# The first norms of a streaming-encoder layer: token sums by one-column matmuls instead of 512-column ones and VectorE additions

## The chip, the cores and the metric

The kernel runs on one core of a Trainium2 chip. The metric is the device time of one execution in microseconds. Three runs of the kernel before took 2073.66 (the median), 2082.34 and 2072.43 us.

## The reference

One layer on 1024 tokens of width 1024, all in float32. It is a first gated feed-forward block, a mixing block (latent attention beside an RWKV-7 recurrence) and a second feed-forward block, each ahead of it with a norm that is modulated by a conditioning vector, and a last norm. What matters here is the start:

```python
mod = silu(c) @ w_mod + b_mod                  # 9 vectors of 1024: sh1, sc1, gt1, ...
u = modulate(rmsnorm(x, ffn1_norm_g), sh1, sc1)
h = x + 0.5 * gt1 * swiglu(u, ffn1_w_gate, ffn1_w_up, ffn1_w_down)

rmsnorm(x, g):  x * rsqrt(mean(x * x, over the 1024 channels) + 1e-6) * g
modulate(u, shift, scale):  u * (1 + scale) + shift
```

The norm needs one number per token: the root of the mean square over the channels.

## The kernel before

Activations lie with channels on the partitions: 8 tiles of 128 channels (index d), each cut into two halves of 512 tokens (index a). So the sum of squares of a token runs over the 128 partitions of eight tiles, and its reciprocal root, to be multiplied in, must stand on all partitions: as "rows", 128 x 512, the same in every partition.

**First half (a = 0), `root` from line 1712.** For each tile ScalarE squares it (L1723) and TensorE multiplies the 512 columns of squares by a 128x128 matrix of ones (L1724), adding up in one PSUM bank. The result is the sum of every token on all partitions at once. ScalarE takes the root of the 128x512 (L254), VectorE its reciprocal (L255, 128x512); that is the rows. The squares turn in four scratch tiles (f8 to f11).

**Second half (a = 1).** `SumSq` squares each tile on ScalarE (L204) and adds six of the eight squares into an accumulator on VectorE (L208). `token_sums` (L216) then takes 128 tokens at a time as the stationary operand of a matmul with one column of ones, for the accumulator and the last square: the sums come out one token per partition, as 128x4. Root and reciprocal are on 128x4. `spread` (L221 to L232) multiplies the identity with them (L226, 128x512 on VectorE), lets TensorE multiply that by the ones (L230), and ScalarE copies the result to SBUF (L231): rows again.

**Rows at work, `norm_raw` (L312).** Even tiles are normalized by VectorE (L320) and then ScalarE (L321), odd ones by POOL (L317) and then ScalarE (L318). Each tile is then split into a high and a low part (L61 on ScalarE, L62 on VectorE), and these are the operands of the first feed-forward products (L68). The weights of these products are split in the same way.

**Modulation.** Scale and shift of the first two tiles come from TensorE (`mod_first`, L152 to L163: 32 matmul instructions with a single stationary column, a copy of the row by ScalarE, and its transposition by L160). Those of the other six tiles come from VectorE, one multiplication of 128x1024 for each of twelve vectors (`mod_one`, L140), on tiles of w_mod that DMA brings. `gain` (L186) makes the factor of a tile.

PSUM scratch called "norm" is drawn from banks 6 and 7 in turn. The tile "nr", which holds the rows, has one buffer: the rows of the second half can be written once those of the first are used up.

**Order.** The engines execute in program order, each its own. That order is written when the kernel is built: a planner takes the instructions by their place in the program and by their times in a simulated timeline. Waits are set from the tiles that instructions share.

Of the kernel before, what the change touches and what calls it, by code (L numbers as in the profile page):

```python
# [13 lines left out]
F32 = mybir.dt.float32  # L14
# [3 lines left out]
ALU = mybir.AluOpType  # L18
AX = mybir.AxisListType
# [3 lines left out]
P = 128  # L23
D = 1024
S = 1024
HB = 512
ND = D // P
# [50 lines left out]
def ps(k, name):  # L78
    b = next(k.bank[name])
    return k.psum.tile([P, HB], F32, name="ps_" + name, tag=f"bank{b}", bufs=1)  # L80
# [8 lines left out]
def spare(slots):  # L89

    return itertools.cycle([(*s, D)[:3] for s in slots])
# [14 lines left out]
def vectors(k, pool):  # L106

    nc = k.nc
    k.pv, k.bmod = (k.const.tile([P, k.I[n].shape[1]], F32, name=n) for n in ("pv", "b_mod"))
    nc.scalar.dma_start(out=k.pv, in_=k.I["pv"])  # L110
    nc.scalar.dma_start(out=k.bmod, in_=k.I["b_mod"])
    k.ccol = k.const.tile([P, ND], F32, name="ccol")
    nc.scalar.activation(out=k.ccol, in_=vec(k, "c"), func=AF.Silu)
# [97 lines left out]
def token_sums(k, parts, t, n=HB):  # L211

    for b in range(n // P):
        c = slice(b * P, (b + 1) * P)
        for i, x in enumerate(parts):
            k.nc.tensor.matmul(  # L216
                t[:, b : b + 1], lhsT=x[:, c], rhs=k.ones[:, 0:1], start=i == 0, stop=i == len(parts) - 1
            )


def spread(k, r, bank, out):  # L221

    nc = k.nc
    m = r.shape[1]
    ident = k.ident[:, None, :].broadcast_to([P, m, P])
    nc.vector.tensor_tensor(  # L226
        out=out.rearrange("p (b q) -> p b q", q=P), in0=ident, in1=r[:, :, None].broadcast_to([P, m, P]), op=ALU.mult
    )
    t = ps(k, bank)[:, : m * P]
    nc.tensor.matmul(t, lhsT=k.ones, rhs=out, start=True, stop=True)  # L230
    nc.scalar.copy(out=out, in_=t)  # L231
    return t  # L232
# [19 lines left out]
def root_mean(k, t, n, out):  # L252

    k.nc.scalar.activation(out=out, in_=t, func=AF.Sqrt, scale=1.0 / n, bias=k.eps)  # L254
    k.nc.vector.reciprocal(out=out, in_=out)  # L255


def rstd(k, pool, ss):

    t = ps(k, "norm")  # L260
    m = ss.n // P
    token_sums(k, ss.parts, t, ss.n)
    r = pool.tile([P, 4], F32, name="rt", tag="rt", bufs=2)[:, :m]
    root_mean(k, t[:, :m], D, r)
    rows = pool.tile([P, HB], F32, name="nr", tag="nr", bufs=1)[:, : ss.n]
    return spread(k, r, "norm", rows), rows
# [21 lines left out]
def empty():  # L288
    return [[None, None] for _ in range(ND)]
# [13 lines left out]
def h_tiles(k, pool, a, out, singles=0):  # L303

    for d in range(singles):
        out[d][a] = pool.tile([P, HB], F32, name=f"h{d}_{a}", tag=f"h{d}_{a}")
    for d in range(singles, ND, 2):
        t = pool.tile([P, 2, HB], F32, name=f"h{d}_{a}", tag=f"h{d}_{a}")
        out[d][a], out[d + 1][a] = t[:, 0], t[:, 1]
# [1349 lines left out]
def tile_layer(ctx, tc, I, out):  # L1659
    k = Ctx()  # L1660
    setup(ctx, k, tc, I, out)
    nc = k.nc
# [10 lines left out]
    with pool_("ffn1") as pool:  # L1673
        fs = [(pool, f"f{i}") for i in range(12)]
        h0, h1 = [(pool, f"h{d}_0") for d in range(0, ND, 2)], [(pool, f"h{d}_1", HB) for d in range(6)]
        wide = [(pool, "e"), (pool, "h6_1")]
        k.wide = spare(us)
        k.spare = spare(fs[8:])
        h = empty()
        u = {}  # L1680

        def load_x(a):
            h_tiles(k, pool, a, h, 6 * a)
            for d in range(ND):
                nc.sync.dma_start(out=h[d][a], in_=I["x"][d, :, a * HB : (a + 1) * HB])

        vectors(k, pool)
        load_x(0)
        early = 2
        slices = {}  # L1690

        def load_mods(ds):
            for d in ds:
                for v in (1, 0):
                    if d < early:
                        w = slices[v, d] = tmp(k, "wmod", D)
                        nc.sync.dma_start(out=w.rearrange("p (i q) -> p i q", q=P), in_=I["w_mod_in"][v * ND + d])
                    else:
                        slices[v, d] = mod_loads(k, v, d)

        def mods(d):
            if d < early:
                mod_first(k, d, [slices[v, d] for v in range(2)])
            else:
                for v in (1, 0):
                    mod_one(k, v, d, slices[v, d])
            gain(k, "ffn1_norm_g", 1, slice(d, d + 1))

        load_mods(range(early))
        slots = iter(fs + us)  # L1710

        def root(a):

            if a:
                ss = SumSq(k, pool, nc.vector)
                for d in range(ND):
                    ss.add(h[d][a])
                r = rstd(k, pool, ss)
                return r
            t = ps(k, "norm")  # L1720
            for d in range(ND):
                sq = tmp(k, "nsq")
                nc.scalar.activation(out=sq, in_=h[d][a], func=AF.Square)  # L1723
                nc.tensor.matmul(t, lhsT=k.ones, rhs=sq, start=d == 0, stop=d == ND - 1)  # L1724
            r = pool.tile([P, HB], F32, name="r", tag="nr", bufs=1)
            root_mean(k, t, D, r)
            return r, r

        def normed(a, r):
            for d in range(ND):  # L1730
                if a == 0 and d >= early:
                    mods(d)
                norm_raw(k, r, h[d][a], d, "ffn1_norm_g", 0)
            return [h[d][a] for d in range(ND)]

        r0 = root(0)
        for d in range(early):
            mods(d)
        x = []

        def first_half():
            spread_c(k, pool)
            load_mods(range(early, 4))
            load_x(1)
            load_mods(range(4, ND))
            x.append(normed(0, r0))
            stream_first(k, u, x[0], slots)

        def second_half():
            x.append(normed(1, root(1)))  # L1750
            stream_second(k, u, x[1], us[8:])

        def both():
            stream_sums(k, u, *x, iter(fs[8:] + us))
            k.spare, k.wide = spare(h1), spare(wide)

        def turn(g):
            if g < 0:
                k.spare = spare(wide + h1)
                return  # L1760
            if g == 0:
                banks(k, dn="67012345")
                for a in range(2):
                    load_x(a)
            if g == 3:
                banks(k, in0="012", dn_in1="34", in2="5", norm="67")
                k.spare = spare(fs[8:])

        steps1 = mod_steps(
            k, (2, lambda: half_gate(k, 2)), (4, lambda: gain(k, "mix_norm_g", 4)), (3, None),  # L1770
            (5, None), (7, lambda: gain(k, "ffn2_norm_g", 7)), (6, None), (8, lambda: half_gate(k, 8)),
        )
        steps1 += trig_steps(k, 0) + trig_steps(k, 1)
        steps2 = []

        u2 = empty()
        places = [us[4:12], us[12:] + us[:4]]

        def then(a, r):
            u_tiles(k, places[a], a, u2)  # L1780
            norm_mod(k, pool, r, h, a, "mix_norm_g", 3, u2)
            for d in range(ND):
                nc.sync.dma_start(out=k.hD[a][:, d, :], in_=h[d][a])

        n2 = Normed(k, pool, h, then)
        first, ws = [[], []], []

        def ahead(a, tiles):

            for i in tiles:  # L1790
                if a == 0:
                    ws.append(win_weights(k, pool, I["w_in"][WIN_FIRST[i]], (("raw", 4), ("wo", 8), ("wo", 8))))
                first[a].append(win_mm(k, ws[i], u2, a, "in0" if a == 0 else ("in1", "in1", "in2")[i]))

        ffn(
            k, u, h, I["ffn1_w_gate"], I["ffn1_w_up"], I["ffn1_w_down"], k.mod[:, 2, :], pool, groups(fs, us),
            itertools.chain([wide[0], us[7]], itertools.cycle(h0)), (lambda: None, lambda: (first_half(), second_half()), lambda: None, both), turn, steps1, steps2,
            n2.final, n2.done, [(0, WHOLE), (1, WHOLE)], ahead,
        )
# [33 lines left out]
    with pool_("inv", "left") as ip, pool_("chain") as pool:  # L1833
# [9 lines left out]
        for p in range(NP2):  # L1843
            o = ops.pop(0)
            even, odd, norm, gate = outputs(k, pool, o)
# [25 lines left out]
    h, y, u = empty(), empty(), {}  # L1871
# [3 lines left out]
    pool = Pools((own("h2b"), h0), (own("w2"), ("raw", "f8", "f9", "f10", "f11", "nwy", "nwt")))  # L1875
    us, fs = [(up, f"u{i}") for i in range(16)], [(pool, f"f{i}") for i in range(12)]
# [122 lines left out]
```

## Time and profile before

| | us |
|---|---|
| median of three runs | 2073.66 |
| the profiled execution | 2078.46 |
| its span, first to last instruction | 2076.7 |
| TensorE busy (matmuls) | 1984.3 (96%) |
| VectorE busy | 1537.3 (74%) |
| ScalarE busy | 889.3 (43%) |
| POOL busy | 250.0 (12%) |
| mean granted clock of TensorE | 0.984 |

PE is TensorE's matmuls, PEld its weight loads, DVE is VectorE, ACT ScalarE, POOL GpSimd, SP the engine that issues most DMAs. Of the profiled execution 2076.7 us lie between the first and the last instruction, and the rest is around them. In the profile a float32 matmul stands as two MATMUL and two LDWEIGHTS instructions. Matmuls overlap in the pipeline, so the distance between the starts of two tells more than the duration of one.

### The profile page before, as it was taken

The numbers are of one execution on the slowest core, as the hardware profiler recorded it, in microseconds if no ns is written. First come the engines' busy times: TensorE is split into PE (matmuls) and PEld (weight loads), VectorE is DVE, ScalarE is ACT, GpSimd is POOL, SyncE is SP. The second block draws the span as 40 slices with busy tenths as digits, with TensorE's granted clock in tenths as the row PEclk, the third lists the DMA queues.
The fourth block names the chain that finished last, engine by engine and source line by source line (L and its number), as shares of the span: only waits on it lengthen the run. The fifth ranks groups of instructions, "written<-read, shape, count | busy, mean of one in ns | idle before, by whom it ended". The sixth has DMA issues, their size and how long they took to land.

```text
span 2076.7 us, 29461 instructions
## 1 busy us (share of the span) xinstructions
PE 1984.3 (96%) x10648; PEld 1597.9 (77%) x10648; DVE 1537.3 (74%) x2939; ACT 889.3 (43%) x1678; POOL 250.0 (12%) x287
## 2 busy tenths in 40 slices
PE   6999999998999999999978999999999999989998
PEld 4788888886888877767767787787888888868887
DVE  6999997668996577887665766568566656689975
ACT  5643334344443364543344444455333333344433
POOL 1100000000000244442132323211000000000001
PEclk8999999999999999999998999999999999999999
DMA  8277753247442224566448874741223323474412
GB/s 337 85 247 241 259 172 122 107 168 233 153 159 90 76 56 115 147 152 152 99 90 174 185 185 133 258 152 51 81 77 112 117 76 111 156 256 152 142 62 82
DMA packets 224658, 302.12 MB, mean 145 GB/s; under 512 B 104704, under 2 KB 138880, under 8 KB 224512
## 3 DMA queue, kind: packets, MB, share of 16 engines
q1 hardware_dynamic: 199888, 288.55, 44.5%
q10 hardware_dynamic: 22064, 4.35, 1.2%
q0 software_dynamic: 2560, 7.34, 1.1%
q8 instruction: 84, 1.38, 0.3%
q14 instruction: 62, 0.51, 0.1%
HBM read 216.81 MB, written 80.74 MB: 143 GB/s over the span
## 4 chain that ended last, share of the span: by engine, by line
PE 74%; DVE 12%; DMA 7%; issue 3%; ACT 2%; POOL 1%; SPq 1%; ACTq 0%; DVEq 0%; POOLq 0%
PE ps_w L68 38%; PE ps_dn L68 19%; PE ps_in L68 5%; PE ps_wo L68 3%; DVE pair L62 2%; PE ps_s L68 1%; PE ps_ov L1264 1%; DVE Tpr L1355 1%; DVE T L1359 1%; DMA hraw<-hidD 1%; PE ps_y L1509 1%; PE ps_z L1475 1%; DVE wmod L140 1%; PE ps_pt L1256 1%; DMA T<-fD 0%
## 5 line engine op out<-in xcount | busy, mean ns | idle before, releaser
L68 PE MATMUL ps_w<-pair 128*128 128x512 f32 x3744 | 873.5, 394 | 13.5 <-ACT pair L61 10.7
L68 PEld LDWEIGHTS ps_w<-pair 128*128 128x128 f32 x3744 | 704.4, 188 | 179.8 <-ACT pair L61 12.1
L68 PE MATMUL ps_dn<-pair 128*128 128x512 f32 x1512 | 357.4, 398 | 15.9 <-DVE h L560 12.9
L68 PEld LDWEIGHTS ps_dn<-pair 128*128 128x128 f32 x1512 | 287.6, 191 | 84.6 <-DVE h L560 14.6
L68 PE MATMUL ps_in<-pair,win 128*128 128x512 f32 x960 | 239.8, 402 | 3.7 <-ACT pair L282 2.2
L61 ACT CAST pair<-raw 128x512 fp32r<-128x512 f32 x256 | 153.7, 621 | 177.5 <-PE ps_w L68 95.9
L68 PEld LDWEIGHTS ps_in<-pair,win 128*128 128x128 f32 x960 | 178.3, 189 | 52.8 <-issue 10.4
L62 DVE TENSOR_TENSOR pair<-raw,pair 128x512 fp32r<-128x512 f32 x256 | 175.9, 700 | 40.1 <-ACT pair L61 39.9
L560 DVE SCALAR_TENSOR_TENSOR h<-ps_dn,mod,h 128x512 f32<-128x512 f32 (+1 forms) x208 | 149.5, 729 | 55.1 <-PE ps_dn L68 50.6
L390 ACT COPY part<-ps_w 128x512 f32<-128x512 f32 x120 | 70.3, 586 | 212.4 <-PE ps_w L68 197.7
L61 ACT CAST pair<-draw 128x256 fp32r<-128x256 f32 x216 | 80.0, 404 | 135.2 <-PE ps_dn L68 66.3
L61 ACT CAST pair<-hraw 128x512 fp32r<-128x512 f32 x142 | 86.3, 619 | 65.8 <-PE ps_dn L68 36.3
L62 DVE TENSOR_TENSOR pair<-hraw,pair 128x512 fp32r<-128x512 f32 x142 | 96.6, 689 | 10.5 <-ACT pair L61 10.2
L208 POOL TENSOR_TENSOR nacc<-nacc,nsq 128x512 f32<-128x512 f32 x12 | 17.7, 1473 | 649.2 <-ACT nsq L204 649.2
L492 DVE TENSOR_TENSOR t<-ps_w,part 128x512 f32<-128x512 f32 x80 | 54.0, 688 | 55.7 <-ACT part L390 45.9
L62 DVE TENSOR_TENSOR pair<-draw,pair 128x256 fp32r<-128x256 f32 x216 | 85.8, 423 | 10.8 <-ACT pair L61 10.7
L140 DVE SCALAR_TENSOR_TENSOR wmod<-wmod,cact 128x1024 f32<-128x1024 f32 x68 | 83.1, 1223 | 3.4 <-DMA wmod<-w_mod 2.9
L68 PE MATMUL ps_dn<-pair,dh 128*128 128x512 f32 (+1 forms) x320 | 83.7, 350 | 0.0
L703 POOL TENSOR_TENSOR h<-h,nr 128x256 f32<-128x256 f32 (+1 forms) x6 | 5.4, 918 | 648.2 <-ACT nr L231 648.2
L487 DVE TENSOR_TENSOR c<-ps_w,part 128x512 f32<-128x512 f32 x80 | 53.6, 687 | 39.9 <-ACT part L390 33.2
L68 PE MATMUL ps_wo<-pair,woh 128*128 128x512 f32 x256 | 80.4, 396 | 0.0
L488 ACT ACTIVATE c<-c 128x512 f32<-128x512 f32 x80 | 49.1, 630 | 31.8 <-DVE c L487 31.0
(350 smaller groups left out, 2795.4 us busy)
## 6 DMA issues: line engine op xcount, KB each, us to landing
wmod<-w_mod SPq DMA_DIRECT2D x68, 512.0 KB, 4.5
raw<-ffn_w_gate SPq DMA_DIRECT2D x44, 512.0 KB, 4.3
raw<-ffn_w_up SPq DMA_DIRECT2D x44, 512.0 KB, 4.3
hidD<-c SPq DMA_DIRECT2D x44, 512.0 KB, 3.8
draw<-ffn_w_down SPq DMA_DIRECT2D x44, 512.0 KB, 5.3
hraw<-hidD SPq DMA_DIRECT2D x72, 256.0 KB, 3.3
h<-x SPq DMA_DIRECT2D x32, 256.0 KB, 5.3
hD<-h SPq DMA_DIRECT2D x32, 256.0 KB, 2.0
```

The costliest lines, as they stand in the source:

```text
L61: k.nc.scalar.copy(out=hi, in_=src)
L62: k.nc.vector.tensor_tensor(out=lo, in0=src, in1=hi.bitcast(F32), op=ALU.subtract)
L68: k.nc.tensor.matmul(out, lhsT=x, rhs=y, start=start, stop=stop, skip_group_check=onto)
L140: k.nc.vector.scalar_tensor_tensor(out=w, in0=w, scalar=1.0, in1=k.cact, op0=ALU.mult, op1=ALU.mult, accum_out=m)
L390: nc.scalar.copy(out=t, in_=x)
L487: nc.vector.tensor_tensor(out=c[i][:, j], in0=x, in1=y, op=ALU.add)
L488: nc.scalar.activation(out=c[i][:, j], in_=c[i][:, j], func=AF.Silu)
L492: nc.vector.tensor_tensor(out=t, in0=x, in1=y, op=ALU.add)
L560: nc.vector.scalar_tensor_tensor(out=y, in0=x, scalar=gt[:, d : d + 1], in1=y, op0=ALU.mult, op1=ALU.add)
L1256: nc.tensor.transpose(tp[:, q : q + P], pr[:, s0 + q : s0 + q + P], k.ident)
L1264: nc.tensor.matmul(x.po[:, cols], lhsT=pt[:, b * P : (b + 1) * P], rhs=k.v[b][:, cols], start=b == 0, stop=b == x.i)
L1355: nc.vector.tensor_tensor(out=v, in0=T[:, t, 0:m][:, None, :].broadcast_to([P, n, m]), in1=xp[:, t, m:][:, :, None].broadcast_to([P, n, m] ...
```

## The change

In both halves, TensorE takes each square as the stationary operand, 128 tokens at a time, with one column of ones, and writes the sum of tile d and token block b to its own column of a 128x4x8 scratch. VectorE adds up the eight columns of each block (one reduction to 128x4). Root and reciprocal are on 128x4, and `spread` makes the rows. In the first half the squares have eight scratch tiles (f0 to f7) of their own, and both consumers read the rows from SBUF.

```diff
         def root(a):
 
-            if a:
-                ss = SumSq(k, pool, nc.vector)
-                for d in range(ND):
-                    ss.add(h[d][a])
-                r = rstd(k, pool, ss)
-                return r
-            t = ps(k, "norm")
+            t = ps(k, "norm")[:, : 4 * ND].rearrange("p (b d) -> p b d", d=ND)
+            if a == 0:
+                k.spare, later = spare(fs[:8]), k.spare
             for d in range(ND):
                 sq = tmp(k, "nsq")
                 nc.scalar.activation(out=sq, in_=h[d][a], func=AF.Square)
-                nc.tensor.matmul(t, lhsT=k.ones, rhs=sq, start=d == 0, stop=d == ND - 1)
-            r = pool.tile([P, HB], F32, name="r", tag="nr", bufs=1)
-            root_mean(k, t, D, r)
-            return r, r
+                for b in range(4):
+                    nc.tensor.matmul(
+                        t[:, b, d : d + 1], lhsT=sq[:, b * P : (b + 1) * P], rhs=k.ones[:, 0:1], start=True, stop=True
+                    )
+            r = pool.tile([P, 4], F32, name="rt", tag="rt", bufs=2)
+            nc.vector.tensor_reduce(out=r, in_=t, axis=AX.X, op=ALU.add)
+            root_mean(k, r, D, r)
+            rows = pool.tile([P, HB], F32, name="nr", tag="nr", bufs=1)
+            t = spread(k, r, "norm", rows)
+            if a == 0:
+                k.spare = later
+            return (t, rows) if a else (rows, rows)
```

## Rows read from the trace of the kernel before

**Rows 1.** Windows: start:end, us, PE, PEld, DVE, ACT, POOL busy, clock, DMA, GB/s.

```profile
25.00:30.00 5.00, 0.91 (x2) 0.82 (x3) 5.00 (x10) 1.34 (x2) 0.75 (x1) 0.51 1.05 389
...
29.10:65.60 36.50, 29.68 (x116) 22.29 (x116) 34.72 (x73) 20.72 (x34) 5.58 (x4) 0.87 0.49 195
...
66.00:2076.00 2010.00, 1937.24 (x10444) 1565.48 (x10442) 1488.82 (x2854) 849.95 (x1617) 236.44 (x266) 0.99 0.46 142
```

**Rows 2.** Chain of waits, 0 to 140 us: start, us, what; first and last of TensorE's.

```profile
4.96 8.67 PE ps_norm L1724 x16
...
65.67 74.35 PE ps_w L68 x316
```

**Rows 3.** Timeline of the first half's norm: start, us, engine, line, operation, idle before.

```profile
13.54 3.65 PE L152 MATMUL ps_norm<-wmod,ccol 128*1 128x128 f32 x32
13.69 1.28 ACT L254 ACT_TABLE_LOAD   x1 [2.85 <-PE ps_norm L1724]
15.71 3.35 DVE L255 RECIPROCAL r<-r 128x512 f32<-128x512 f32 x1 [15.71 <-ACT r L254]
...
19.21 6.54 POOL L317 TENSOR_TENSOR h<-h,r 128x512 f32<-128x512 f32 x4 [17.15 <-DVE r L255]
...
22.50 0.60 PE L160 MATMUL ps_norm<-ones,row 1*128 1x1 f32 x4 [0.51 <-ACT row L157]
...
26.89 0.74 DVE L320 SCALAR_TENSOR_TENSOR h<-h,gs_ffn_norm_g,r 128x512 f32<-128x512 f32 x1
...
28.76 0.15 DVE L163 TENSOR_TENSOR mod<-ps_norm,b_mod 128x2 f32<-128x2 f32 x1
```

**Rows 4.** Weight loads of line L1724, before 8.2 us and after: min/median/max ns.

```profile
L1724 PEld LDWEIGHTS ps_norm<-nsq,ones x5: 288/338/338, 4.9 to 7.7; 128*128 128x128 f32 x5
...
L1724 PEld LDWEIGHTS ps_norm<-nsq,ones x11: 190/190/192, 8.3 to 12.6; 128*128 128x128 f32 x11
```

**Rows 5.** Timeline of one-column matmuls, the third and the last pair; then windows.

```profile
43.09 0.36 PE L216 MATMUL ps_norm<-ones,nsq 128*128 128x1 f32 x2
...
44.43 0.36 PE L216 MATMUL ps_norm<-ones,nsq 128*128 128x1 f32 x2
...
25.20:25.60 0.40, 0.00 (x0) 0.00 (x0) 0.40 (x1) 0.00 (x0) 0.40 (x1) 0.50 1.01 399
45.00:45.40 0.40, 0.00 (x0) 0.00 (x0) 0.40 (x5) 0.09 (x1) 0.00 (x0) 1.00 1.04 399
45.80:46.20 0.40, 0.00 (x0) 0.00 (x0) 0.40 (x1) 0.00 (x0) 0.00 (x0) 0.50 0.91 369
```

**Rows 6.** VectorE's groups, by shape, 0 to 70 us (reduction: whole span).

```profile
L62 DVE TENSOR_TENSOR pair<-raw,pair 128x512 fp32r<-128x512 f32 x8 | 8.2, 1066 | 0.0
L62 DVE TENSOR_TENSOR pair<-h,pair 128x512 fp32r<-128x512 f32 x12 | 8.1, 683 | 1.2 <-ACT pair L61 1.2
...
L255 DVE RECIPROCAL rt<-rt 128x4 f32<-128x4 f32 x1 | 0.2, 177 | 0.0
...
L1235 DVE TENSOR_REDUCE st<-ps_s 128x1 f32<-128x128 f32 x8 | 2.3, 290 | 0.2
...
L208 DVE TENSOR_TENSOR nacc<-nacc,nsq x6: 684/690/693, 35.8 to 40.9; 128x512 f32<-128x512 f32 x6
```

**Rows 7.** ScalarE's groups of the second half's norm, 0 to 70 us.

```profile
L231 ACT COPY nr<-ps_norm 128x512 f32<-128x512 f32 x1 | 0.6, 587 | 0.5 <-PE ps_norm L230 0.5
...
L254 ACT ACTIVATE rt<-ps_norm,eps 128x4 f32<-128x4 f32 x1 | 0.3, 263 | 2.9 <-PE ps_norm L216 2.9
```

**Rows 8.** Timeline of TensorE, 40 to 90 us.

```profile
48.60 7.52 PE L68 MATMUL ps_w<-pair 128*128 128x512 f32 x24 [3.81 <-ACT pair L61]
...
55.96 1.02 PE L230 MATMUL ps_norm<-nr,ones 128*128 128x512 f32 x2
```

**Rows 9.** Timeline of SP's queue, and its w_mod transfers (KB, median us to landing).

```profile
28.53 5.06 SPq L133 DMA_DIRECT2D wmod<-w_mod  x8
...
wmod<-w_mod SPq DMA_DIRECT2D x8, 512.0 KB, 8.1
```

## Prediction

> **What bounds the kernel now.** I read the engines' busy time by stage first, then the chain of waits, then the timeline of the first 70 us. Behind 66 us TensorE is busy 1937 of 2010 us; ahead of it there are holes (0.91 us of work in 25 to 30) and VectorE is the full engine, 34.7 of the 36.5 us before the long run [rows 1]. The chain agrees: it goes through TensorE for the first norm's sums, then through VectorE with short turns on ScalarE, and at 65.67 TensorE starts a run of 316 matmuls without a break [rows 2]. The change lies wholly ahead of 65.67, and after that the kernel is paid in TensorE's time. So the question is only when that run can start. The profiled execution took 2078.46 us (span 2076.7); the median of the three runs, 2073.66, is 4.8 us lower. I work the sum against the profiled one and carry the difference over.
>
> **First half, the sums.** Removed: 16 TensorE instructions of 512 columns (two per fp32 matmul), 4.96 to 13.63 us [rows 2]. Added: 8 tiles x 4 matmuls x 2 = 64 pairs of a 128x128 weight load and a one-column matmul. The only such pairs of this stage are the second norm's token sums: 12 of them start between 43.09 and 44.43, so 0.112 us a pair [rows 5], at the full clock. At that rate the sums last 7.2 us and end at 12.1. But the engine starts at half clock: the same weight load took 338 ns before 8.2 us and 190 ns after [rows 4], and what raised the clock was a stretch of 512-column matmuls. What one-column matmuls do to it is seen once: after the burst to 44.8 the clock was still full at 45.0 to 45.4 and half at 45.8 to 46.2 [rows 5], about a microsecond after the engine stopped at 44.8, while the half clock of 25.2 came 2 us after it had stopped at 23.1 [rows 3, 5]. So they did not hold the clock up, and I expect that they don't raise it. Then a pair costs 0.112 x 338/190 = 0.199 us, 64 of them 12.7, and the sums end at 17.7. Ends: 12.1, and 19.3 (0.224, twice the fast rate). I take 17.7, by the row of the same weight load at half clock: 4.1 us later than now.
>
> The Trainium skill ("TensorE: Matmul & The Clock Gate", section Part 1, the HAM clock gate) says that activity releases the throttle and idleness brings it back. Read plainly, a stream of pairs is activity: the clock would rise at about 8 us as now, and the sums would end near 13.5 (15 pairs at 0.199 by 8 us, 49 at 0.112). The rows of the burst at 43 us speak against it; it is the first rival. The same page's section LDWEIGHTS (loading the stationary operand) times a load by its columns over 1.2 GHz, a time in which the gate does not appear; by it the pairs would run at the fast rate throughout and end at 12.1. The 338 against 190 ns contradict that.
>
> **First half, root to rows.** Now: table load 1.28 at 13.69, the root, a reciprocal of 3.35, and POOL starts at 19.21, 5.6 us after the sums [rows 2, 3]. Then: a small reduction on VectorE that this trace does not have; the nearest row is the reduction of 128 PSUM columns, 0.29, the floor is the 128x4 reciprocal at 0.18; I take 0.2 [rows 6]. Table load 1.28, root on 128x4 0.26, reciprocal 0.18, product with the identity 0.69 (as an addition of this size), spreading matmul 1.02, copy 0.59 [rows 3, 6, 7, 8]: 4.2, with handovers 4.6. That is only 1 us less than now, for the 3.35 us reciprocal is replaced by a longer row of steps. Rows are ready at 22.3 if TensorE takes the spreading matmul at once. It will probably have begun the 32 modulation matmuls of tile 0 (3.65 us at full clock [rows 3], 6.5 at half by the ratio of rows 4): then 23 to 26.
>
> **The first modulations.** The "norm" banks alternate between 6 and 7. One more scratch is drawn in the first norm, so the second scratch of tile 0's modulation now falls on the bank that holds the spread root: its transposing matmuls wait for the copy of the rows. Today that modulation waits for VectorE, which is held by the reciprocal until 19.06 and then by eight weight splits that POOL's multiplications beside them stretch to 1.07 us each, against 0.68 [rows 6]. After the change VectorE is free at 17 and does the eight splits alone, 8 x 0.68 = 5.5 us, before POOL starts; that is what hides the later root. If that cover is gone, because the splits are queued on VectorE behind the reduction, the reciprocal or the product, each of which now waits for TensorE or ScalarE, they start at 20.6 instead of 18.98 (17.7 + 0.2 + 1.28 + 0.26 + 0.18 + 0.69 and handovers): all that follows is 1.6 us later, but POOL's cost stays on the splits as now, so that VectorE comes out about the same either way. The first normalized tile, now at 26.89 [rows 3], comes at 24 to 27.8; I take 26.9, no change, and the first product, 2.2 us behind it, likewise. Tile 1 fares worse: behind tile 0's transposition come 3.65 us of matmuls, a copy and a transposition, so its modulation is there at about 31 instead of 28.76 at the latest [rows 3]. Half of that can be filled with other VectorE work: +1.5 us. POOL's four multiplications (6.54 us [rows 3]) now lie beside later VectorE work and stretch that instead: +2 us (0 to 3.1, the 8 x 0.38 that they cost the splits now).
>
> **Second half on VectorE.** Removed: six additions, 4.1 us [rows 6], and a wait of 0.4; added: one reduction of 0.2. The root on 128x4, product and spreading are there already. VectorE's balance at 65 us: +1.5 + 2 - 4.3 = -0.8 (-3.5 to +3). The tiles of w_mod, of which VectorE works off twelve in this stretch, hold it little: the last eight are issued in 28.53 to 33.6 and land a median 8.1 us behind, so by some 43 [rows 9], 22 us before the run.
>
> **Second half on TensorE.** 16 pairs become 64: 7.2 us for 1.8, so +5.4 at full clock, +10.9 at half. Cover: the idle 3.81 us before the products at 48.60 [rows 8]. (TensorE's other gaps between 29.1 and 65.6 are 3.0 us together [rows 1]; I count 0.6 of them ahead of that point.) What is left, 1 us (to 6.5 at half clock), moves these products and with them the spreading matmul (55.96), which is queued behind them and on which the whole second half's norm waits; from there to the run at 65.67 the steps stay as they are. Also, ScalarE's squares turn in four buffers that VectorE's additions set free and that TensorE's matmuls would; behind a square that waits stand the casts that TensorE needs. I cost this at nothing since the additions free them only between 35.8 and 41.6 now [rows 6], when TensorE is there as well; the other end is 1 us. So TensorE, not VectorE, sets the run: +1 us.
>
> **Sum.** 2078.46 + 1 = 2079.5 for the profiled execution, 2074.7 by the median. No change that a measurement of this kernel can tell; 0.5%, about 10 us, is what it can.
>
> **Rivals.**
> 1. The clock rises with one-column work, or the pairs run at 0.112 anyway. Then the sums end at 12 to 14, the reciprocal's net 2.3 us (3.35 less 0.69, 0.18 and 0.2) and the additions' 4.1 both come out of VectorE's chain: -6.2; TensorE's own load (29.7 us in the 36.5 before the run [rows 1], plus 5.4, from a start 2.3 earlier, with 1 us of gaps) ends at 62.9, which allows only -3. For it: VectorE is the chain throughout. Against: the half-clock load and the fall of the clock [rows 4, 5]. Between them: -4.5, 2069.2.
> 2. Slower: the second half's 64 pairs run at half clock and stand together ahead of the products at 48.60. 12.7 us instead of 1.8, less 4.4 of cover, is +6.5, and the late modulation of tile 1 adds 1.5: +8, 2081.7. It decides where the products of tiles 4 and 5 start after 51 us instead of 48.6. For it: the half clock after the burst at 43 us. Against: the squares come one by one, as the additions do [rows 6], so the pairs can lie between 512-column products that keep the clock.
> 3. The order of the instructions behind 66 us is written by a planner from modelled times. A shifted start can turn some choices there. TensorE has 73 us of idle time behind 66 us [rows 1]; a tenth of that either way is 7 us: 2068 or 2082. Nothing in the profile says which.
>
> **Chances.** Forecast (within 4 us of 2074.7) 0.50, rival 1 0.18, rival 2 0.20, rival 3 0.12. The range for 8 in 10 takes in rivals 1 and 2 with their ends: 2066 to 2084. Faster by over 0.5% (under 2063.3) needs rival 1 and rival 3 together: 0.06. Slower (over 2084.0) needs rival 2 at its upper end or with rival 3: 0.12. The rest, 0.82, is no change.
>
> **What would show it.** Right: the weight loads of the first sums at about 0.34 us throughout, sums ending near 18 us, reciprocal gone from VectorE and the eight splits at 0.68 each before POOL's first multiplication; no additions in 35 to 41; TensorE without its gap before 48; the long run starting at 65 to 68 us. Wrong: sums over by 14 us at full clock (rival 1), or the products of tiles 4 and 5 behind 51 us (rival 2), or a run that starts as I say and a total that doesn't follow it (rival 3).

## The result: slower by 0.9%, and the profile after

The changed kernel takes 2092.72 us (median of four runs, 2091.41 to 2098.13) against 2076.05 for the kernel before on the same chip (four runs, 2072.43 to 2082.34): a ratio of 1.0087, with a 95% interval of 1.0070 to 1.0103. The forecast was no change (2074.7), in a range that ended at 2084. The profiled execution is the slowest of the four, 2098.13 us (span 2096.3, mean granted clock 0.977), 19.7 us above that of before.

Windows of the kernel after, in the columns of [rows 1]:

```profile
29.10:65.60 36.50, 29.87 (x126) 26.14 (x124) 27.21 (x60) 18.11 (x29) 5.93 (x5) 0.67 0.50 197
66.00:2076.00 2010.00, 1945.10 (x10418) 1569.11 (x10417) 1481.26 (x2833) 848.52 (x1611) 238.58 (x266) 0.98 0.46 140
```

VectorE, the full engine before, is relieved as meant: 27.2 us of the 36.5 instead of 34.7. But the mean granted clock of TensorE in this stretch fell from 0.87 to 0.67, and the stretch got longer. The timeline of the kernel after (start, us, engine, line, operation, idle before) shows the first half's norm, to be read against [rows 3]:

```profile
4.83 13.78 PE L1721 MATMUL ps_norm<-ones,nsq 128*128 128x1 f32 x64 [4.83 <-ACT nsq L1719]
...
17.39 1.98 DVE L62 TENSOR_TENSOR pair<-raw,pair 128x512 fp32r<-128x512 f32 x3 [17.39 <-ACT pair L61]
19.29 0.18 DVE L1725 TENSOR_REDUCE rt<-ps_norm 128x4 f32<-128x32 f32 x1
...
19.52 5.94 PE L152 MATMUL ps_norm<-wmod,ccol 128*1 128x128 f32 x32 [0.91 <-DVE rt L1725]
...
22.09 0.18 DVE L255 RECIPROCAL rt<-rt 128x4 f32<-128x4 f32 x1 [0.81 <-ACT rt L254]
...
25.39 1.13 PE L230 MATMUL ps_norm<-nr,ones 128*128 128x512 f32 x2
...
26.56 0.59 ACT L231 COPY nr<-ps_norm 128x512 f32<-128x512 f32 x1 [0.69 <-PE ps_norm L230]
...
27.29 6.98 POOL L317 TENSOR_TENSOR h<-h,nr 128x512 f32<-128x512 f32 x4 [25.23 <-ACT nr L231]
...
29.38 0.60 PE L160 MATMUL ps_norm<-ones,row 1*128 1x1 f32 x4
...
35.54 0.15 DVE L163 TENSOR_TENSOR mod<-ps_norm,b_mod 128x2 f32<-128x2 f32 x1
...
36.41 0.75 DVE L320 SCALAR_TENSOR_TENSOR h<-h,gs_ffn_norm_g,nr 128x512 f32<-128x512 f32 x1
...
37.36 1.00 PE L160 MATMUL ps_norm<-ones,row 1*128 1x1 f32 x4 [6.63 <-ACT row L157]
```

The sums end at 18.6 instead of 13.6, the modulation matmuls behind them take 5.94 us instead of 3.65, and the rows are ready at 27.2. Tile 0 is then normalized at 36.4 instead of 26.9, for its modulation (L163) stands on VectorE at 35.5, behind other modulations (L140) and behind tile 2, though its transposition (L160) was done at 30.0. TensorE has nothing to run for the 6.63 us ahead of 37.36. What follows stands in the chain of waits, which now runs through TensorE for the second half (start, us, what):

```profile
37.36 1.00 PE ps_norm L160 x4
38.36 6.92 PE ps_norm L1721 x32
45.28 1.92 PE ps_w L68 x4
47.20 1.50 PE ps_norm L1721 x8
48.69 1.49 PE ps_w L68 x3
50.18 4.91 PE ps_norm L1721 x24
55.09 8.19 PE ps_w L68 x28
63.28 0.87 PE ps_norm L230 x2
```

All 64 pairs of the second half (L1721) stand among the first seven products (L68 x4, x3), 32 of them ahead of the first, whose operand VectorE had written at 36.5; it starts at 45.1 instead of 29.1. And all of it runs at half clock. Weight loads of L1721 (min/median/max ns, first and last start), of the first half, and the clock windows of the same kernel, then one window of the kernel before:

```profile
L1721 PEld LDWEIGHTS ps_norm<-ones,nsq x64: 287/333/333, 4.8 to 18.2; 128*128 128x128 f32 x64
...
8.00:12.40 4.40, 4.40 (x22) 4.40 (x22) 0.00 (x0) 2.41 (x5) 0.00 (x0) 1.00 1.02 367
34.40:58.40 24.00, 21.04 (x83) 19.68 (x84) 18.20 (x48) 14.34 (x24) 0.00 (x0) 0.50 0.53 211
```

```profile
34.40:58.40 24.00, 19.58 (x81) 14.83 (x80) 22.22 (x52) 13.46 (x22) 0.72 (x1) 0.86 0.52 207
```

Three things are to be read here. The loads take 333 ns from 4.8 to 18.2 us, the half-clock figure of [rows 4]. The clock column says 1.00 at 8 to 12.4 all the same: the trace's first change of clock, a rise, is at 24.2, and ahead of it the column tells nothing, so the loads decide. And from 34.4 to 58.4 the clock is at half without a break (0.50, which is 1.2 GHz), where before it averaged 0.86. It fell at 34.5, in TensorE's wait ahead of 37.36, so here the pairs did not bring it down; but it did not come up again while they ran, and rose at 58.4, in the products that start at 54.95.

How the loss builds up is counted best by the start of the n-th feed-forward product instruction (the matmuls of tile ps_w, 3744 in either kernel) and of matmuls of later stages, in us. The experiments below stand in the same table:

| kernel | 1st | 50th | 192nd | 1872nd | first ps_in | 1000th ps_dn |
|---|---|---|---|---|---|---|
| before | 29.1 | 49.2 | 88.7 | 477.2 | 703.3 | 1843.4 |
| after | 45.1 | 67.2 | 99.8 | 490.5 | 716.6 | 1862.7 |
| e1, first half changed | 42.7 | 59.2 | 94.4 | 482.0 | 708.3 | 1851.9 |
| e2, second half changed | 29.9 | 56.6 | 93.9 | 482.6 | 706.2 | 1852.5 |
| e3, after, 128 columns | 29.0 | 50.5 | 90.7 | 478.6 | 704.4 | 1850.5 |
| e4, after, own banks | 37.9 | 61.8 | 94.4 | 481.1 | 707.0 | 1850.0 |
| e5, before, one instruction more | 29.1 | 49.8 | 89.9 | 478.7 | 701.9 | 1839.5 |
| e6, second half, 128 columns | 30.0 | 50.3 | 89.7 | 477.8 | 702.3 | 1839.1 |
| e7, first half, 128 columns | 29.0 | 47.3 | 88.8 | 477.1 | 702.0 | 1843.9 |
| e8, first half, row sums | 31.2 | 52.2 | 93.7 | 482.5 | 705.4 | 1848.0 |
| e9, after, 128 columns, own banks | 26.3 | 49.3 | 87.1 | 474.7 | 699.0 | 1838.8 |

After minus before: 16.1 us at the first product, 18.0 at the 50th, and 11.1 at the 192nd, since the kernel before has waits of its own behind 48 us where the kernel after already runs without a break. 2.2 more come by the 1872nd product, and 6.0 between the first ps_in and the 1000th ps_dn. The first stage is the larger part, and it is what the runs were made to explain. Each row is a single execution, and the four runs of the kernel before differ by 9.9 us among themselves; so differences of a few us in the late columns carry little by themselves.

### The profile page after: what moved, and what is told of

Same layout as the page of the kernel before. It is cut to its first block, busy times and chain, and to the rows that moved or that the text cites. A ratio compares the mean times of both kernels' runs of the same rounds, so it can differ in the third digit from the quotient of the medians.

```text
span 2096.3 us, 29647 instructions
## 1 busy us (share of the span) xinstructions
PE 2009.4 (96%) x10746; PEld 1625.2 (78%) x10746; DVE 1529.2 (73%) x2936; ACT 890.2 (42%) x1679; POOL 250.9 (12%) x287
## 4 chain that ended last, share of the span: by engine, by line
PE 67%; DVE 14%; DMA 10%; issue 4%; ACT 3%; POOL 1%; SPq 1%; ACTq 0%; DVEq 0%; POOLq 0%
PE ps_w L68 30%; PE ps_dn L68 19%; PE ps_in L68 6%; PE ps_wo L68 4%; DVE pair L62 3%; DMA wmod<-w_mod 2%; DVE wmod L140 2%; PE ps_s L68 1%; PE ps_ov L1264 1%; DMA m<-m3D 1%; DMA raw<-ffn_w_gate 1%; DVE T L1359 1%; DMA draw<-ffn_w_down 1%; DVE Tpr L1355 1%; PE ps_y L1509 1%
## 5 line engine op out<-in xcount | busy, mean ns | idle before, releaser
L68 PE MATMUL ps_w<-pair 128*128 128x512 f32 x3744 | 871.5, 394 | 2.4 <-ACT part L390 0.9
L68 PEld LDWEIGHTS ps_w<-pair 128*128 128x128 f32 x3744 | 702.8, 188 | 167.3 <-ACT part L390 1.9
L68 PE MATMUL ps_dn<-pair 128*128 128x512 f32 x1512 | 358.5, 398 | 14.0 <-DVE h L560 8.2
L68 PEld LDWEIGHTS ps_dn<-pair 128*128 128x128 f32 x1512 | 288.0, 191 | 83.5 <-DVE h L560 9.9
L68 PE MATMUL ps_in<-pair,win 128*128 128x512 f32 x960 | 242.5, 405 | 4.6 <-ACT pair L282 2.2
L68 PEld LDWEIGHTS ps_in<-pair,win 128*128 128x128 f32 x960 | 180.6, 192 | 54.4 <-issue 10.4
L61 ACT CAST pair<-hraw 128x512 fp32r<-128x512 f32 x142 | 86.7, 619 | 59.6 <-PE ps_dn L68 29.4
L492 DVE TENSOR_TENSOR t<-ps_w,part 128x512 f32<-128x512 f32 x80 | 53.9, 686 | 59.9 <-ACT part L390 49.2
L140 DVE SCALAR_TENSOR_TENSOR wmod<-wmod,cact 128x1024 f32<-128x1024 f32 x68 | 84.0, 1237 | 12.0 <-DMA wmod<-w_mod 10.8
L68 PE MATMUL ps_dn<-pair,dh 128*128 128x512 f32 (+1 forms) x320 | 84.3, 352 | 0.0
L68 PE MATMUL ps_wo<-pair,woh 128*128 128x512 f32 x256 | 80.2, 395 | 0.0
```

Source lines behind the costliest of these rows:

```text
L61: k.nc.scalar.copy(out=hi, in_=src)
L68: k.nc.tensor.matmul(out, lhsT=x, rhs=y, start=start, stop=stop, skip_group_check=onto)
L140: k.nc.vector.scalar_tensor_tensor(out=w, in0=w, scalar=1.0, in1=k.cact, op0=ALU.mult, op1=ALU.mult, accum_out=m)
L492: nc.vector.tensor_tensor(out=t, in0=x, in1=y, op=ALU.add)
```

## The experiments

Theory: one-column matmuls leave TensorE at half clock, which lengthens both halves' sums and whatever follows them. Rivals: one half alone bears the loss; the place of the work (the shared bank, the order of the queues) costs it, whatever the clock does; any shift of the order costs as much behind the stage. Ratios below are against the kernel before on the same chip, with 95% intervals.

**Each half alone (e1, e2).** The kernel after with the old `root` for one of the halves.

```diff
+        def root(a):
+            return (root_second if a else root_first)(a)
```

In e1 `root_first` is the new one and `root_second` the old one, in e2 the other way round.

> Only the first half's norm is changed; the second half keeps ScalarE's squares with VectorE's additions. Theory A (both halves cost, each in its own way): the first half's 64 pairs run at half clock to about 18.6 us, the modulation of tile 0 comes behind the spreading matmul and behind VectorE's work for tiles 2 and 3, and the first 512-column product starts near 40 us instead of 29.1; by the end of the first 192 products 5 to 7 of the 11 us are lost. Total +6 to +10 us. Rival B (the second half's pairs, which stand ahead of the first product, are the whole cost): the first products start by 32 us and the total is within 3 us of before.

> Only the second half's norm is changed; the first half keeps its 512-column sums. Theory A: the first product starts at 29 us as before, the one-column pairs stand between products and hold the engine up by 3 to 5 us, partly at half clock; VectorE is 4 us lighter and gives 1 to 2 of it back. Total +2 to +5 us. Rival B (the second half is the whole cost): +10 us or more by the 192nd product. Rival C (removing the additions pays when the first half is left alone): -2 to -4 us.

e1: 2088.18 us, ratio 1.0043 (1.0028 to 1.0058). e2: 2086.90 us, 1.0032 (1.0022 to 1.0042). At the 192nd product e1 is 5.7 us late and e2 5.2, together 10.9 of the 11.1: the two halves bear the loss of this stage about equally and add up. That one of them bears it alone is refuted. The total of e2, by its ratio some 6.7 us over before, is above the 2 to 5 that were expected. e1 repeats the start of the kernel after (modulation matmuls at half clock, timeline of TensorE):

```profile
19.93 6.29 PE L152 MATMUL ps_norm<-wmod,ccol 128*1 128x128 f32 x32 [1.10 <-DVE rt L1725]
...
42.70 7.14 PE L68 MATMUL ps_w<-pair 128*128 128x512 f32 x16 [3.95 <-ACT pair L61]
```

**The moving operand (e3, e6, e7).** The weight loads stay, the same number of them; each matmul streams 128 columns of ones in place of one. Since these are all ones, every column holds the block's sum, accumulated over the tiles; the reduction adds eight of them, and the mean is taken over eight times the channels.

```diff
-            t = ps(k, "norm")[:, : 4 * ND].rearrange("p (b d) -> p b d", d=ND)
+            t = ps(k, "norm").rearrange("p (b q) -> p b q", q=P)
...
-                        t[:, b, d : d + 1], lhsT=sq[:, b * P : (b + 1) * P], rhs=k.ones[:, 0:1], start=True, stop=True
+                        t[:, b], lhsT=sq[:, b * P : (b + 1) * P], rhs=k.ones, start=(b, d) == (0, 0),
+                        stop=(b, d) == (3, ND - 1), skip_group_check=True,
...
-            nc.vector.tensor_reduce(out=r, in_=t, axis=AX.X, op=ALU.add)
-            root_mean(k, r, D, r)
+            nc.vector.tensor_reduce(out=r, in_=t[:, :, :ND], axis=AX.X, op=ALU.add)
+            root_mean(k, r, D * ND, r)
```

e3 has this in both halves, e6 in the second with the first as before, e7 in the first with the second as before.

> As the changed kernel, but each square block is multiplied by 128 columns of ones instead of one, accumulated over the eight tiles in TensorE (the reduction then adds eight equal columns and the mean divides by eight times as much). Same weight loads, same number of instructions, same steps behind them; only the moving operand is 128 times as long. Theory A (one-column matmuls leave the clock at half): the weight loads of the first sums fall from about 330 to 190 ns from about 8 us on, the sums end near 14 us instead of 18.6 although more is streamed, and the first modulation matmuls of 128 columns run at full clock (3.7 instead of 5.9 us); the total is 4 to 8 us below the changed kernel. Rival (the pair's rate is set by the weight load whatever the clock, or the clock is late for another reason): the sums end at 18 us or later and the total is not below the changed kernel.

> The first half as before; the second half as changed, but with 128 columns of ones instead of one. Beside the run that changed only the second half (50th product at 56.6 us, half clock from 40.5 to 54.2). Theory A (one-column pairs drop the clock, and the products among them run at half): the clock stays full from 34 us on but for a few us, the 50th product comes at 49 to 52 us and the 192nd within 2 us of before (88.7). Rival (the order, with pairs standing between the products, is what costs): the 50th product comes behind 54 us although the clock is full. Total: 3 to 5 us over before under A, since the order behind 110 us changes too; 7 or more under the rival.

> The first half as changed, but with 128 columns of ones; the second half as before with VectorE's additions. Theory A: sums over by 13.6 us, first product at 29 us, VectorE 2.3 us lighter than before for the small reciprocal; the 192nd product within 2 us of before on either side, the total 0 to 6 us above before by the order behind 110 us. Rival (the small reciprocal pays once the clock is kept): the 192nd product 2 us or more ahead of before.

e3: 2084.48 us, 1.0025 (1.0014 to 1.0035). e7: 2080.99, 1.0017 (1.0007 to 1.0028). e6: 2073.58, 0.9974 (0.9960 to 0.9987). In the stage, 128 columns bring back 9.1 of the 11.1 us when in both halves (192nd product at 90.7), 5.6 of 5.7 in the first (88.8 against 94.4 in e1), 4.2 of 5.2 in the second (89.7 against 93.9 in e2). Weight loads of L1721 in 8.3 to 13 us, e3 and then the kernel after:

```profile
L1721 PEld LDWEIGHTS ps_norm<-ones,nsq x44: 192/192/192, 8.2 to 13.0; 128*128 128x128 f32 x44
```

```profile
L1721 PEld LDWEIGHTS ps_norm<-ones,nsq x23: 333/333/333, 8.2 to 12.9; 128*128 128x128 f32 x23
```

In the same stretch TensorE makes 44 weight loads at 192 ns or 23 at 333. (In the second half of e3, 16 products stand ahead of the pairs, which is not so in the kernel after; there the operand is not the only difference.) The timeline of TensorE in e3 has the sums end at 13.56, as before the change, and the modulation matmuls at the full-clock 3.65 us:

```profile
4.76 8.80 PE L1721 MATMUL ps_norm<-ones,nsq 128*128 128x128 f32 x64 [4.76 <-ACT nsq L1719]
13.85 3.65 PE L152 MATMUL ps_norm<-wmod,ccol 128*1 128x128 f32 x32 [0.28 <-DVE rt L1726]
```

The cleanest pair is e2 and e6, for there TensorE's order is nearly line for line the same. TensorE's timeline and two windows of e2, then the same of e6:

```profile
29.95 7.50 PE L68 MATMUL ps_w<-pair 128*128 128x512 f32 x24 [6.09 <-ACT pair L61]
37.28 1.84 PE L1738 MATMUL ps_norm<-ones,nsq 128*128 128x1 f32 x16
...
42.52 6.82 PE L1738 MATMUL ps_norm<-ones,nsq 128*128 128x1 f32 x32
...
51.33 10.68 PE L68 MATMUL ps_w<-pair 128*128 128x512 f32 x40
...
34.40:58.40 24.00, 24.00 (x111) 21.52 (x110) 17.41 (x45) 11.95 (x20) 0.00 (x0) 0.72 0.52 208
40.60:54.00 13.40, 13.40 (x53) 12.38 (x53) 9.51 (x24) 5.40 (x8) 0.00 (x0) 0.50 0.46 181
```

```profile
30.00 7.55 PE L68 MATMUL ps_w<-pair 128*128 128x512 f32 x24 [6.09 <-ACT pair L61]
37.38 1.95 PE L1738 MATMUL ps_norm<-ones,nsq 128*128 128x128 f32 x16
...
41.45 3.73 PE L1738 MATMUL ps_norm<-ones,nsq 128*128 128x128 f32 x32
...
46.29 9.37 PE L68 MATMUL ps_w<-pair 128*128 128x512 f32 x40
...
34.40:58.40 24.00, 24.00 (x137) 20.67 (x136) 19.90 (x49) 14.19 (x23) 1.18 (x1) 1.00 0.53 209
40.60:54.00 13.40, 13.40 (x82) 11.85 (x82) 13.16 (x35) 6.49 (x10) 0.00 (x0) 1.00 0.46 183
```

Both run 24 products and 16 pairs at full clock. Then e2's clock is at half from 40.5 to 54.2 and e6's is not; here no wait stands ahead of the fall, as one does in the kernel after. TensorE is busy for all of the 24 us in both, with 111 instructions in e2 and 137 in e6. 32 pairs take 6.82 us against 3.73, and the products between and behind them are slower too. 128 columns cost little at full clock: 16 pairs take 1.95 us against 1.84. So for the second half's loss in this stage the clock is shown to be the cause, with the order all but held fast. The totals of the two lie 0.0058 of the time apart, some 12 us, of which the stage holds 4.2; the rest lies behind it and is not explained by these windows. e6 was expected 3 to 5 us over before and came out under it. For the first half e1 against e7 shows that the one-column operand is the cause, but not how much of it goes by way of the clock alone, since VectorE's order changed with it (tile 0's L163 at 35.9 in e1, at 26.5 in e7).

**The bank (e4, e9).** The sums and the spread root of the first half get scratch banks 4 and 5, apart from the modulations' 6 and 7, in the kernel after (e4) and in e3 (e9). The products draw from 4 and 5 too, as before.

```diff
-    banks(k, w7="012345", norm="67", dn="67")
+    banks(k, w7="012345", norm="67", dn="67", root="45")
...
-            t = spread(k, r, "norm", rows)
+            t = spread(k, r, ("norm", "root")[a == 0], rows)
```

> As the changed kernel, but the first half's sums and rows draw from PSUM banks 4 and 5 of their own, so that the first modulations don't wait for the bank that holds the spread root. Theory A' (the shared bank is what puts the modulation of tile 0 late): tile 0's modulation is taken by VectorE at 28 to 30 us instead of 35.5, the first product comes 4 to 6 us earlier, and the total is 3 to 6 us below the changed kernel. Rival (TensorE's order and half clock alone): the modulation of tile 0 comes within 2 us of the changed kernel's, and the total is the same within 2 us.

> Both halves as changed, with 128 columns of ones, and the first half's sums and rows in banks 4 and 5 of their own. If the shared bank costs something also with the clock kept (theory A'): tile 0's modulation is taken before 22 us, the first product starts 3 to 5 us ahead of before (29.1), and the 192nd comes at 87 to 89 us, against 90.7 with shared banks; the total is within 4 us of before on either side. If only the clock mattered (rival): the 192nd product comes at 90 to 91 us and the total stays 3 to 6 us above before.

e4: 2090.49 us, 1.0052 (1.0036 to 1.0068). e9: 2077.70, 0.9996 (0.9982 to 1.0010). Timeline of TensorE, the first normalization on VectorE and the group of L163 (first and last start) in e4, then the timeline in e9:

```profile
18.52 6.36 PE L152 MATMUL ps_norm<-wmod,ccol 128*1 128x128 f32 x32
24.80 1.13 PE L230 MATMUL ps_root<-nr,ones 128*128 128x512 f32 x2
25.86 0.60 PE L160 MATMUL ps_norm<-ones,row 1*128 1x1 f32 x4
...
30.10 1.83 DVE L320 SCALAR_TENSOR_TENSOR h<-h,gs_ffn_norm_g,nr 128x512 f32<-128x512 f32 x1
...
L163 DVE TENSOR_TENSOR mod<-ps_norm,b_mod x2: 147/150/153, 26.5 to 36.6; 128x2 f32<-128x2 f32 x2
```

```profile
19.09 0.60 PE L160 MATMUL ps_norm<-ones,row 1*128 1x1 f32 x4
19.62 3.65 PE L152 MATMUL ps_norm<-wmod,ccol 128*1 128x128 f32 x32
26.27 1.60 PE L68 MATMUL ps_w<-pair 128*128 128x512 f32 x4 [3.00 <-ACT pair L61]
```

With banks of its own, tile 0's transposition no longer waits for the copy of the rows: it starts at 25.9 instead of 29.4 and its L163 at 26.5 instead of 35.5, though the sums and the modulation matmuls (6.36 us) run at half clock as in the kernel after. That is worth 5.4 us at the 192nd product (94.4 against 99.8), and 3.6 where the clock is kept (87.1 in e9 against 90.7 in e3). So the bank, with the order that goes with it, is a second cost, and partly the same time seen from another side: 9.1 us come back through the columns, 5.4 through the banks, 12.7 through both. In e9 the stage is 1.6 us ahead of the kernel before: the change's idea does work there. The total says no change.

**Sums as a row (e8).** To have the 128x4 root without one-column pairs: the ones are a single stationary column, the squares the 512 moving ones, and four small matmuls transpose the row of sums. First half alone, second as before, own banks.

```diff
+            t = ps(k, "root")[0:1]
...
+                nc.tensor.matmul(t, lhsT=k.ones[:, 0:1], rhs=sq, start=d == 0, stop=d == ND - 1)
+            row = tmp(k, "row")[0:1]
+            nc.scalar.copy(out=row, in_=t)
...
+                    t[:, b : b + 1], lhsT=row[:, b * P : (b + 1) * P], rhs=k.ones[0:1, 0:1], start=True, stop=True
```

> A version that might beat both: the second half as before; in the first half the 512-column matmuls stay, with one column of ones as the stationary operand, so that the sums stand in one row; ScalarE copies the row, eight small instructions transpose it, root and reciprocal are on 128x4, and the rows are spread as in the second half; banks 4 and 5 of their own. Theory A (the clock is kept, the modulations don't wait, VectorE loses 2.3 us of work): first product at 24 to 28 us, the 192nd product 1 to 3 us ahead of before, the total from -3 to +4 us, for the later order is again another. Rival (the longer chain of small steps eats the gain): the 192nd product no earlier than before.

2081.98 us, 1.0027 (1.0016 to 1.0039); 192nd product at 93.7. Timeline of TensorE, then its windows:

```profile
26.55 1.42 PE L230 MATMUL ps_root<-nr,ones 128*128 128x512 f32 x2
...
37.50 11.58 PE L68 MATMUL ps_w<-pair 128*128 128x512 f32 x43 [5.13 <-DVE pair L62]
...
20.40:27.20 6.80, 5.95 (x25) 3.78 (x26) 5.72 (x11) 5.22 (x9) 0.00 (x0) 0.50 1.03 402
34.00:40.80 6.80, 3.30 (x8) 2.63 (x9) 6.70 (x13) 5.26 (x9) 2.29 (x2) 0.50 1.03 410
68.10:75.00 6.90, 5.02 (x11) 3.64 (x12) 6.90 (x13) 6.89 (x14) 0.00 (x0) 0.51 0.00 0
```

I had expected the row to escape the loss; it does not. The spreading matmul comes at 26.6 in place of 17.4 in e3, after a chain of short steps, TensorE waits 5.13 us ahead of its fifth product, and in these three stretches the clock is at half, with TensorE busy for 5.95, 3.30 and 5.02 us of each. So this run does not tell the clock theory from the others; it shows a third way of making the first half late.

**One instruction more (e5).** The kernel before with one product of 128x512 on VectorE (ones into scratch, used by nothing), to see what a shift of less than a microsecond does to the order behind.

```diff
             stream_second(k, u, x[1], us[8:])
+            pad = tmp(k, "pad").rearrange("p (b q) -> p b q", q=P)
+            ones = k.ones[:, None, :].broadcast_to([P, 4, P])
+            nc.vector.tensor_tensor(out=pad, in0=ones, in1=ones, op=ALU.mult)
```

> The kernel before with a single VectorE instruction more: a 128x512 product of ones into a scratch nobody reads, behind the second half's splits. On the engine it costs 0.69 us at most. Theory (a shifted start makes the planner write another order behind 110 us, and that order is worse by some 3 to 6 us): the 192nd product comes within 1.5 us of before, and the total is 3 to 7 us above it, lost between 700 and 1300 us as in the four earlier runs. Rival (the later loss comes from the new norm itself, its late tiles or its buffers): the total is within 1.5 us of before.

2078.64 us, 1.0011 (1.0000 to 1.0023). That a shift as such costs 3 to 7 us behind the stage is not borne out: the 1872nd product is 1.5 us late and the 1000th ps_dn 3.9 us early. A smaller cost is not excluded, for the interval of the ratio reaches 4.8 us.

**The version that wins, again (e10).** e6 once more, on another chip in five rounds.

> The version that was ahead of the kernel before in one comparison (first half as before, second half with 128 columns of ones), timed again with more rounds. If its gain is one of this kernel: ratio 0.996 to 0.999 again. If it was a chance of one chip and its runs: 0.999 to 1.001.

2071.65 us against 2078.51, 0.9971 (0.9955 to 0.9988). It beats both kernels, the one before by about 0.3% (some 6 us by the ratios; 3.5 and 6.9 by the medians) and the changed one by more. The two timings, on two chips, agree, and so do their traces: the same instruction starts within 0.8 us of itself at every point of the table, and the stretch from the first ps_in to the 1000th ps_dn lasts 1136.8 and 1136.0 us. Why it wins is not shown: its stage is 1.0 us behind the kernel before at the 192nd product, and what it gains lies behind 477 us. The profiled execution of e6 is the slowest of its ten (2076.33), so its trace shows little of the gain.

## Why the prediction was wrong, step by step

**Bound and method.** That VectorE was the full engine was right. That the end is set by when TensorE can start its long run was not (see the run, below).

**First half, the sums: right.** A pair was put at 0.199 us and the end at 17.7; measured are 0.215 (13.78 by 64) and 18.6, at half clock throughout. Rival 1, which rested on a clock that rises, is refuted. The Trainium skill ("TensorE: Matmul & The Clock Gate", section Part 1, the HAM clock gate) says that activity releases the throttle. The trace does not agree, if a stream of pairs is activity: 13.8 us of them without a gap did not release it. The same page of the Trainium skill has a load time without the gate in it (section LDWEIGHTS (loading the stationary operand)). The runs do not agree: the same load takes 192 ns in e3 and 333 in the kernel after.

**Root to rows: right in kind, short by a microsecond.** The case "23 to 26", with the modulation matmuls taken first, came true; the rows were ready at 27.2. The small reduction took 0.18 (0.2 taken), the matmuls at half clock 5.94 (6.5), the reciprocal 0.18. The eight splits ran at 0.68 to 0.69 each ahead of POOL, as foreseen.

**"The first normalized tile ... comes at 24 to 27.8; I take 26.9, no change": failed.** Tile 0 came at 36.4. I had seen the shared bank and priced its wait by the time of the copy alone. What the wait does to the order was left out: the planner put 26 matmuls of tile 1 ahead of tile 0's transposition on TensorE, and modulations and tile 2 ahead of tile 0 on VectorE. The cover, splits done early, was there, and it covered nothing, because the modulation waited for the bank and the order and not for VectorE's splits. In e4, with banks of its own and the first half still at half clock, L163 is at 26.5, but the first normalization on VectorE at 30.1; so at most 6.3 of the 9.5 us come back with the banks. With 128 columns and the bank still shared they come back whole: the first L320 is at 26.8 in e3 and e7, though in both 30 matmuls of tile 1 stand ahead of that transposition. So the bank does not delay tile 0 by itself; it does so together with the late, slow start that the one-column sums make. With the late sums this delay makes the first half's 5.7 us (e1); of these 5.6 go with the one-column operand (e7).

**"Second half on TensorE ... What is left, 1 us": failed, by its size.** The term was given as 1 us, 6.5 at half clock; alone it measures 5.2 (e2). Two things were wrong in the choice of the low end. The argument that pairs between 512-column products keep the clock fell: in e2 they lie between products, and the clock drops at 40.5 and stays at half for 13.7 us, products included. And the cover of 3.81 us of [rows 8] is a gap of the old order; in the new one pairs stand between products (e2), in the kernel after half of them ahead of the first product, whose operand was there at 36.5.

**VectorE's balance** (-0.8) no longer mattered: it is busy 27.2 us where it was 34.7, and what was saved there became idle time, since the chain had moved to TensorE. That ScalarE's squares wait for TensorE came true with four waits, 2.6 us in all.

**The run.** It was to start at 65 to 68 us. By its timeline TensorE does not pause behind 37.36: the run starts 28 us sooner than in [rows 2], and the kernel is slower. The start of a run was the wrong sign for an end, because what the run holds had changed (pairs, and products at half clock). The 192nd product, 11.1 us late, is the sign that holds.

**Rivals.** Rival 2 has the mechanism: pairs at half clock, together, ahead of the products, and products behind 51 us (L68 x28 at 54.95). Its price for them, 6.5 of its 8 us, is near the 5.2 of e2; its chance of 0.20 was too low, and it had not seen that the first half loses as much. Rival 3, the order behind, may add to it: 2.2 us between the 192nd and the 1872nd product, and 6.0 between 703 and 1863 us in the profiled execution. Windows from the first to the 960th ps_in matmul, before and after:

```profile
703.30:1022.70 319.40, 305.59 (x1490) 233.95 (x1490) 234.79 (x340) 149.40 (x239) 108.74 (x117) 0.99 0.48 119
```

```profile
716.60:1040.30 323.70, 309.61 (x1490) 237.48 (x1489) 234.63 (x341) 149.13 (x238) 110.03 (x118) 0.97 0.47 117
```

The same 1490 instructions take 4.0 us more of busy TensorE at a clock of 0.97 instead of 0.99; that goes with most of the 6.0. What makes the clock fall there was not tried. The changed code does not run there, and the same stretch to the 1000th ps_dn lasts 1136.8 to 1146.3 us over the eleven orders of the table, while one order run twice gave 1136.8 and 1136.0. So I take it for an effect of the order that the planner wrote, which is argued and not shown: every other order was profiled once, and chance from run to run is not excluded.

**The sum.** Forecast was +1: nothing for the first half, 1 for the second. At the 192nd product it is 11.1: 5.7 with the first half changed alone and 5.2 with the second. The whole loss is 19.7 us in the profiled execution and 16.7 in the medians; what lies behind the stage, 8.6 or 5.6 of it, stays open.

## What to carry to other kernels

Price a sum by one-column matmuls by its weight loads at half clock, where it can come to stand there, and count the work behind it at half clock with it: ask what the engine's clock will be after the new instructions, not only during them. If such matmuls stand ahead of heavy work, give them a wide moving operand, which here cost 0.11 us on 16 pairs. And where a written order fills gaps, a gap seen in the old trace is no cover for new work: the order is written anew, and the new work may stand ahead of what the gap was waiting for.

## What the runs showed of the hardware that was not expected

TensorE can be busy for all of 24.00 us and have a clock of 0.72 in them (e2), while nearly the same order with 128 columns has 1.00 (e6): here its busy time does not tell its clock. A pair of weight load and one-column matmul costs 0.115 us at full clock and 0.213 to 0.215 at half, and with 128 columns 0.117 to 0.122 at full. Before the first change of clock that a trace records, the clock column can read 1.00 at half clock, as it does at 8 to 12.4 us of the kernel after; a weight load of 333 against 192 ns tells it there.
